# Four tile pools ordered by last use, and an RWKV chunk step in three batches

## The chip, the core and the metric

One core of a Trainium2 chip runs the whole program. The engines are TensorE (PE, with PEld for its weight loads), VectorE (DVE), ScalarE (ACT), GpSimd (POOL) and SyncE (SP, which here issues nearly all DMAs). The metric is the device time of one execution in microseconds; lower is better.

## What is computed

One layer of a bidirectional hybrid trunk, first for a prompt of 256 tokens and then for 2048 latent tokens, in float32:

```python
h = rms_norm(x, p['norm_mix_g']) * (1.0 + scale1) + shift1
(r, k, v, wd_f, wd_b, ad_f, ad_b, gd, xb, gb, q, ff, fb, iv, og) = jnp.split(h @ p['w_in'], idx, axis=-1)
o_a, s_a = rwkv7_mixer(r, k, v, (wd_f, wd_b), (ad_f, ad_b), gd, s_rwkv, p)   # 8 heads of 64, forward + backward
o_b, s_b = rglru_mixer(xb, gb, s_lru, p)
o_c, s_c = hgrn2_mixer(q, (ff, fb), iv, og, s_hgrn, p)
x = x + gate1 * (jnp.concatenate([o_a, o_b, o_c], axis=-1) @ p['w_out'])
h = rms_norm(x, p['norm_ffn_g']) * (1.0 + scale2) + shift2
x = x + gate2 * conv_ffn(h, p, on_grid)          # gated MLP, width-3 depthwise convolution

# inside rwkv7_mixer, per direction and token
s_kk = jnp.einsum('bhvk,bhk->bhv', S, kk_t)
S = (S * w_t[:, :, None, :] - s_kk[..., None] * (kk_t * a_t)[:, :, None, :] + v_t[..., None] * k_t[:, :, None, :])
o_t = jnp.einsum('bhvk,bhk->bhv', S, r_t)
```

The latent tokens start from cached states, the prompt from zero; outputs are both token sets (final RMSNorm) and the prompt's final states.

## The kernel before, in words

The 2304 tokens are 9 pieces of 256: piece 0 is the prompt. **Phase 1** (`dense1`) projects five sections of two pieces (the last has one) with w_in: each weight block of 128 columns is split in a high and a low part (`split`, line 364 on ACT and line 365 on POOL or DVE), and three matmuls (lines 368 to 370, helper `mm3`) make one float32 product. Between its steps a list of lanes runs: generators that issue a few instructions up to their next `yield`. `run` adds a rate per lane to a credit at each step of the dense generator and steps the lane once for each full credit (`RATES` in phase 1, `RATES2` during the prompt's MLP). Lane 1 holds the forward RWKV chain (`rw_fwd`), then the prompt's backward chain and its tail; lane 5 holds the backward chain of pieces 8 to 6; lane 0 the per-head preparation and later the tails (`rw_tail`: group norm, gate, and a store of the mixed rows to DRAM as dMX). Lane 4 solves the triangular systems of a section (`rw_solve`).

An RWKV chunk is 64 tokens for 8 heads (4 pairs). `rw_loads` reads its operands: ar (two buffers), bk and tt (one buffer each), uv (two). `rw_chunk` then runs five batches, each ended by a yield: the Gram matmuls of bk with ar and their masking into gm (lines 743 to 750; the copy at line 747 on POOL); the transposes of bk (line 756), copied to bt by ACT; z (line 768); u (line 775); the new state (line 782, DVE lines 784 and 785) with the output (lines 789 to 796). `in_order` keeps the PE instructions of one chunk in this order. The operands of the next chunk are loaded at the beginning of a chunk. There are 36 forward and 36 backward chunks; those of the prompt's and the latent pieces 8 to 6 run before the second phase, the backward chunks of pieces 5 to 1 inside it, on lane 0 at rate 1. In the backward chain of pieces 8 to 6 the tiles go by other names (`ALT`: ar is k, bk is r, uv is v, gm is hft1, bt is est), and their PSUM tiles too.

Then the prompt's output projection and MLP run (`dense2([(0, 1)])`, with DN["late"] set), and **phase 2**, `dense2(SEC2)`, does the same for pieces 6 to 8, 3 to 5 and 1 to 2. For a section of three pieces the tokens are two halves of 384. Each half loads the mixed rows (`mixin`, m<-dMX, line 1436), the rows of x (`xin`, line 1446) and, quarter by quarter, w_out (`rows_w`, line 1453), which DVE multiplies by the gate g1 (line 1455) and which is split; products are added to x at line 1479.

Instruction order is fixed when the program is built: a scheduler places instructions on each engine's queue by priority and by a simulated time line, and a tile's memory is waited for tile by tile. Pools are stacks from two sides. On the right, phase 1 has cp1, mpa and mpb (the tags of `LATE` go to mpb); after them phase 2 puts gp2 (gate g1), ha2 (high, low and x tiles of the first half), wp2 (split weights, three deep) and rp2 (raw weights and m, three deep) over the same memory. On the left stand the weights and tiles of the prompt's MLP, and then hp2 (gates g2 and fg, MLP tiles), mp2 and hb2 of phase 2.

Of the kernel before, what the change touches and what calls it, by code (L numbers as in the profile page):

```python
# [10 lines left out]
F32 = mybir.dt.float32  # L11
# [46 lines left out]
RATES = (1.2, 1.0, 0.8, 0.6, 0.8, 1.2)  # L58
RATES2 = (1.5, 2.0, 2.0, 1.0, 2.0, 3.0)
# [42 lines left out]
def build(tc, a, o):  # L102
# [9 lines left out]
    NCH = NT // 64  # L112
# [296 lines left out]
    cp, mpa, mpb = [pool(p1, nm, "right") for nm in ("cp1", "mpa", "mpb")]  # L409
    lp = pool(pd1, "lp1", "left")  # L410

    class mp:

        LATE = {"AR", "BK", "t1", "t2", "t3", "hft0", "gst", "gs2", "gs3", "k", "r", "v", "hft1", "est", "hg1", "hH0",
                "S1", "kk", "t4", "lw0", "lw1", "la0", "la1"}

        @staticmethod
        def tile(shape, dt, tag, bufs, name):
            return (mpb if tag in mp.LATE else mpa).tile(shape, dt, tag=tag, bufs=bufs, name=name)

# [307 lines left out]
    def rw_chunk(bp, d, c, ld, Sin, emit_o, tg={}):  # L728

        def tl(tag, shape):  # L730
            tag, bufs = tg.get(tag, (tag, 1))
            return bp.tile(shape, F32, tag=tag, bufs=bufs, name=tag)
# [4 lines left out]
        ar, bk, tt, uv = ld  # L737
        H = (slice(0, 64), slice(64, 128))
        last = None
# [5 lines left out]
        gm = tl("gm", [128, 4, 2, 128])  # L745
# [6 lines left out]
        yield  # L752
        pb = [pt("eo"[h], [128, 4, 64]) for h in range(2)]
        for p in range(4):
            for h in range(2):
                last = in_order(last, T.transpose(pb[h][:, p, :], bk[H[h], p, :, :].rearrange("r a x -> r (a x)"),
                                                  ident[H[h], H[h]]))
        bt = tl("bt", [128, 4, 2, 64])
        for h in range(2):
            S.copy(bt[:, :, h, :], pb[h])  # L760
        yield
# [23 lines left out]
        V.tensor_tensor(S1, S1, WC[d][c // 8][:, c % 8, :].unsqueeze(2).to_broadcast([128, 4, 64]), op=ALU.mult)  # L785

# [21 lines left out]
    def rw_fwd(q):  # L808

        yield from until(lambda: (2 * (q // 2), 0) in solved)  # L810
        if q == 0:
            s0 = mp.tile([128, 4, 64], F32, tag="S0", bufs=2, name="S0")
            V.memset(s0, 0.0)
            rwF["S"] = [s0]
            rwF["ld"] = rw_loads(mp, 0, 0)
            yield
        elif q == 1:
            st = rw_state_in(mp, 0)
            rw_final(mp, 0, rwF["S"])
            yield  # L820
            rwF["S"] = [rw_flip(mp, st, "S0")]
            yield
        for ci in range(4):
            c = 4 * q + ci
            ld = rwF["ld"] if rwF.get("ld") else rw_loads(mp, 0, c)
            rwF["ld"] = rw_loads(mp, 0, c + 1) if ci < 3 else None

            def emit_o(po):
                ob = mt("mv", (128, 4, 64), 1)
                S.copy(ob, po)  # L830
                S.dma_start(dOF[q][ci], ob.rearrange("r p x -> r (p x)"))
            yield from rw_chunk(mp, 0, c, ld, rwF["S"], emit_o)
# [416 lines left out]
    def rw_bwd(q):  # L1249
# [15 lines left out]
        ld = rw_loads(BG["pool"], 1, 4 * q + 3, tg)  # L1265
        for ci in (3, 2, 1, 0):
            cur, ld = ld, (rw_loads(BG["pool"], 1, 4 * q + ci - 1, tg) if ci else None)
# [3 lines left out]
            yield from rw_chunk(BG["pool"], 1, 4 * q + ci, cur, rwB["S"], emit_o, tg)  # L1271
# [300 lines left out]
    def dense2(secs, between):  # L1572
# [14 lines left out]
        for i, (q0, n) in enumerate(secs):  # L1587
# [61 lines left out]
            DN.update(ps=both)  # L1649
            bump(part=0)  # L1650
# [137 lines left out]
    gp, ha, wp2, rp2 = [pool(p2, nm, "right") for nm in ("gp2", "ha2", "wp2", "rp2")]  # L1788
# [6 lines left out]
    for nm, j in (("g1", 16), ("g2", 40), ("fg", None)):  # L1795
        DN[nm] = gate_rows([(gp if nm == "g1" else hp2).tile([128, 512], F32, name=f"{nm}{f}") for f in range(2)], j, 1)
# [45 lines left out]
```

## Time and profile before

| what | value |
|---|---|
| median of three runs | 3950.99 us (3948.19 to 3953.86) |
| the profiled execution | 3953.64 us, span of its trace 3951.8 us |
| PE busy | 3652.6 us, 92% of the span |
| DVE, ACT, POOL busy | 2466.2, 1597.5, 1186.0 us |
| mean granted clock of TensorE | 0.959 |

Busy time is the sum over an engine's instructions. A granted clock of 1 is 2.4 GHz and of 0.5 is 1.2 GHz; a value between is the mean of a stretch. "Idle before, releaser" is the time that an engine stood still before an instruction and whose end let it go on. A wait on SP's queue is time in which a DMA issue stood at the head of that queue.

### The profile page before, as it was taken

What the parts mean: (1) busy time and instruction counts of PE and PEld (TensorE: products, weight loads), DVE (VectorE), ACT (ScalarE), POOL (GpSimd) and SP (SyncE); (2) the same over time, 40 slices, a digit from 0 to 9 for tenths busy, and PEclk for the clock granted to TensorE, in tenths of its full rate; (3) what the DMA queues carried; (4) which work ended last, traced back from release to release, by engine and by line L of the source; (5) the groups of instructions that cost most, each with busy time, mean ns of one, the idle gap of its engine ahead of it and who ended that gap; (6) DMA issues with size and microseconds to landing.
All of it is one profiled execution on the core that took longest, in us unless ns stands there. A gap on an engine that the chain in (4) does not pass through costs nothing.

```text
span 3951.8 us, 74642 instructions
## 1 busy us (share of the span) xinstructions
PE 3652.6 (92%) x29752; PEld 3055.7 (77%) x29752; DVE 2466.2 (62%) x4623; ACT 1597.5 (40%) x2840; POOL 1186.0 (30%) x808
## 2 busy tenths in 40 slices
PE   5998999989999997799867999999999999999998
PEld 3776777766777785688746888998778999979998
DVE  4667777576667677856678455353765433376665
ACT  4456345444554656444333222222342222243333
POOL 2441221202021021334433333333333333343332
PEclk8999999989999997899988999999999999999999
DMA  7988977777877888666464232222522222242332
GB/s 255 305 271 267 271 228 242 241 205 212 248 237 221 268 273 255 200 175 190 122 210 128 85 91 78 74 83 65 173 75 64 71 65 65 64 144 81 97 91 81
DMA packets 769538, 649.10 MB, mean 164 GB/s; under 512 B 247258, under 2 KB 647974, under 8 KB 768166
## 3 DMA queue, kind: packets, MB, share of 16 engines
q1 hardware_dynamic: 736790, 610.10, 51.0%
q10 hardware_dynamic: 32400, 34.22, 2.8%
q8 instruction: 235, 3.85, 0.4%
q14 instruction: 113, 0.93, 0.1%
HBM read 481.08 MB, written 163.10 MB: 163 GB/s over the span
## 4 chain that ended last, share of the span: by engine, by line
PE 47%; DVE 7%; DMA 3%; issue 2%; ACT 1%; POOL 0%; SPq 0%; ACTq 0%; DVEq 0%; POOLq 0%
PE mm L368 6%; PE mm L369 6%; PE mm L370 6%; PE xh L368 6%; PE xh L369 5%; PE xh L370 5%; PE e L368 1%; PE e L369 1%; PE e L370 1%; DVE raw L1455 1%; PE o L369 1%; DVE x L1479 1%; PE o L370 1%; PE o L368 1%; DVE tm L1559 1%
## 5 line engine op out<-in xcount | busy, mean ns | idle before, releaser
L365 POOL TENSOR_TENSOR wlo<-raw,whi 128x1024 fp32r<-128x1024 f32 x273 | 666.5, 2443 | 972.5 <-ACT whi L364 680.1
L368 PE MATMUL mm<-hhi,whi 128*128 128x512 f32 (+2 forms) x2224 | 801.5, 361 | 25.2 <-ACT whi L364 8.5
L369 PE MATMUL mm<-hlo,whi 128*128 128x512 f32 (+2 forms) x2224 | 788.8, 355 | 8.0 <-DVE hlo L286 5.6
L370 PE MATMUL mm<-hhi,wlo 128*128 128x512 f32 (+2 forms) x2224 | 785.5, 353 | 2.0 <-DVE wlo L365 1.0
L364 ACT CAST whi<-raw 128x1024 fp32r<-128x1024 f32 x333 | 348.3, 1048 | 717.5 <-PE mm L370 319.2
L368 PEld LDWEIGHTS mm<-hhi,whi 128*128 128x128 f32 x2224 | 427.8, 193 | 84.1 <-issue 13.3
L369 PEld LDWEIGHTS mm<-hlo,whi 128*128 128x128 f32 x2224 | 428.2, 193 | 51.8 <-DVE hlo L286 6.3
L370 PEld LDWEIGHTS mm<-hhi,wlo 128*128 128x128 f32 x2224 | 427.5, 192 | 45.9 <-POOL wlo L365 2.1
L365 POOL TENSOR_TENSOR alo<-gs,ahi 128x384 fp32r<-128x384 f32 (+1 forms) x154 | 150.4, 977 | 445.0 <-ACT ahi L364 431.6
L368 PE MATMUL xh<-hhi,whi 128*128 128x384 f32 (+1 forms) x824 | 274.5, 333 | 4.5 <-ACT hhi L364 4.5
L369 PE MATMUL xh<-hlo,whi 128*128 128x384 f32 (+1 forms) x824 | 272.6, 331 | 3.2 <-DVE hlo L365 2.6
L370 PE MATMUL xh<-hhi,wlo 128*128 128x384 f32 (+1 forms) x824 | 272.6, 331 | 0.0
L1675 DVE SCALAR_TENSOR_TENSOR gs<-xh,vec,gs 128x378 f32<-128x378 f32 (+1 forms) x103 | 60.8, 590 | 318.2 <-ACT gs L1671 318.2
L1479 DVE TENSOR_TENSOR x<-xh,x 128x512 f32<-128x512 f32 x220 | 150.5, 686 | 88.9 <-PE xh L370 85.1
L1479 DVE TENSOR_TENSOR x<-mm,x 128x512 f32<-128x512 f32 x172 | 118.1, 687 | 108.9 <-PE mm L370 107.1
L747 POOL COPY gm<-ar 64x256 f32<-64x256 f32 x120 | 58.2, 485 | 391.5 <-PE c L792 301.4
L1455 DVE TENSOR_TENSOR raw<-raw,g 128x1024 f32<-128x1024 f32 x98 | 127.3, 1299 | 76.3 <-DMA raw<-in_ffn_w_down 67.5
L365 POOL TENSOR_TENSOR t<-t,t 128x512 fp32r<-128x512 f32 (+1 forms) x40 | 53.0, 1325 | 388.0 <-ACT t L364 301.2
L1681 DVE SCALAR_TENSOR_TENSOR gs<-fsg,gs 128x384 f32<-128x384 f32 (+1 forms) x154 | 122.6, 796 | 71.4 <-ACT fsg L1680 71.1
L368 PEld LDWEIGHTS xh<-hhi,whi 128*128 128x128 f32 x824 | 156.0, 189 | 8.0 <-ACT hhi L364 4.8
L369 PEld LDWEIGHTS xh<-hlo,whi 128*128 128x128 f32 x824 | 155.8, 189 | 5.2 <-DVE hlo L365 2.9
L370 PEld LDWEIGHTS xh<-hhi,wlo 128*128 128x128 f32 x824 | 155.9, 189 | 0.7
(607 smaller groups left out, 8415.9 us busy)
## 6 DMA issues: line engine op xcount, KB each, us to landing
whi<-dW SPq DMA_DIRECT2D x116, 512.0 KB
wlo<-dW SPq DMA_DIRECT2D x116, 512.0 KB
raw<-in_ffn_w_gate SPq DMA_DIRECT2D x88, 512.0 KB
raw<-in_ffn_w_up SPq DMA_DIRECT2D x88, 512.0 KB
raw<-in_ffn_w_down SPq DMA_DIRECT2D x88, 512.0 KB
x<-in_x_sample SPq DMA_DIRECT2D x44, 512.0 KB
raw<-in_w_out SPq DMA_DIRECT2D x40, 512.0 KB
dAR<-AR SPq DMA_DIRECT2D x32, 512.0 KB
```

The costliest lines, as they stand in the source:

```text
L364: S.copy(hi, raw)
L365: e.tensor_tensor(lo, raw, hi.bitcast(F32), op=ALU.subtract)
L368: T.matmul(out, whi, xhi, start=first, stop=False)
L369: T.matmul(out, whi, xlo, start=False, stop=False)
L370: T.matmul(out, wlo, xhi, start=False, stop=last)
L747: G.tensor_copy(gm[H[h], :, h, 0:64], ar[H[h], :, 0, :])
L1455: V.tensor_tensor(raw, raw, g[f].unsqueeze(1).to_broadcast([128, 2, 512]), op=ALU.mult)
L1479: V.tensor_tensor(x1b[:, FS[f]], pt, x1b[:, FS[f]], op=ALU.add)
L1559: V.tensor_scalar(t[:, 128 * i:128 * i + 128], pt[:, 128 * i:128 * i + 128], A2[:, k, c:c + 1], mod[:, 24 + k, c:c + 1], op0=ALU.mult, op1 ...
L1675: V.scalar_tensor_tensor(gv[:, :, 1:rw], pv[:, :, 0:rw - 1], cw(0), gv[:, :, 1:rw], op0=ALU.mult, op1=ALU.add)
L1681: V.scalar_tensor_tensor(gs[:, :w], sg[:, :w], 1.0, gs[:, :w], op0=ALU.add, op1=ALU.mult)
```

## The change

- The pools of phase 1 on the right become cp1, mpa (`EARLY`), mpd (`JOIN`), mpc (`CHAIN`) and mpb (the rest). Phase 2's right-hand pools are opened in the order gp2, rp2, wp2, ha2.
- The gates g2 and fg of phase 2 are loaded by `mlp_gates`, called after the first output projection of phase 2; g1 is loaded where it was.
- A chunk step has three batches: transposes, S copies and z; u; new state, the Gram of the next chunk (`rw_gram` on the head `nxt`), output. The first chunk of a chain, or one whose successor's section is not solved when it begins, has its Gram in a batch of its own. `nxt` may belong to the next piece, except in phase 2.
- The transposes are four of 128 by 128 into one PSUM bank, copied by one ACT instruction, instead of eight of 64 rows into two banks and two copies.
- The rates of lanes 1 and 5 are three fifths of what they were.

```diff
-RATES = (1.2, 1.0, 0.8, 0.6, 0.8, 1.2)
-RATES2 = (1.5, 2.0, 2.0, 1.0, 2.0, 3.0)
+RATES = (1.2, 0.6, 0.8, 0.6, 0.8, 1.2)
+RATES2 = (1.5, 1.2, 2.0, 1.0, 2.0, 1.8)
...
-    cp, mpa, mpb = [pool(p1, nm, "right") for nm in ("cp1", "mpa", "mpb")]
+    cp, mpa, mpd, mpc, mpb = [pool(p1, nm, "right") for nm in ("cp1", "mpa", "mpd", "mpc", "mpb")]
...
+        EARLY = {"ar", "bk", "tt", "uv", "gm", "bt", "mv", "S0", "Dn", "m4", "hq", "ep", "hg0", "hS", "nss", "ls", "lhl"}
+        JOIN = {"hK", "hQ", "hF", "hA", "hH1", "hl", "hVt", "hv", "hg64"}
+        CHAIN = {"k", "r", "v", "hft1", "est", "hg1", "hH0", "S1"}
...
-            return (mpb if tag in mp.LATE else mpa).tile(shape, dt, tag=tag, bufs=bufs, name=name)
+            p = mpa if tag in mp.EARLY else mpd if tag in mp.JOIN else mpc if tag in mp.CHAIN else mpb
+            return p.tile(shape, dt, tag=tag, bufs=bufs, name=tag)
...
+    def rw_head(bp, d, c, tg={}):
+
+        return {"ld": rw_loads(bp, d, c, tg), "c": c}
...
+    def rw_turn(bp, hd, last, tg):
+
+        tl, pt = rw_tiles(bp, tg)
+        bk = hd["ld"][1]
+        pb = pt("e", [128, 4, 128])
+        for p in range(4):
+            last = in_order(last, T.transpose(pb[:, p, :], bk[:, p, :, :].rearrange("r a x -> r (a x)"), ident))
+        hd["bt"] = tl("bt", [128, 4, 2, 64])
+        S.copy(hd["bt"].rearrange("r p h x -> r p (h x)"), pb)
+        return last
+
+    def rw_gram(bp, d, hd, last, tg):
...
-        yield
-        pb = [pt("eo"[h], [128, 4, 64]) for h in range(2)]
-        for p in range(4):
-            for h in range(2):
-                last = in_order(last, T.transpose(pb[h][:, p, :], bk[H[h], p, :, :].rearrange("r a x -> r (a x)"),
-                                                  ident[H[h], H[h]]))
-        bt = tl("bt", [128, 4, 2, 64])
-        for h in range(2):
-            S.copy(bt[:, :, h, :], pb[h])
-        yield
+        return last
+
+    def rw_chunk(bp, d, hd, nxt, Sin, emit_o, tg={}):
...
+        if "gm" not in hd:
+            last = rw_gram(bp, d, hd, last, tg)
+            yield
+        last = rw_turn(bp, hd, last, tg)
+        gm, bt = hd["gm"], hd["bt"]
         S0 = Sin[0]
...
         V.tensor_tensor(S1, S1, WC[d][c // 8][:, c % 8, :].unsqueeze(2).to_broadcast([128, 4, 64]), op=ALU.mult)
+        if nxt is not None:
+            last = rw_gram(bp, d, nxt, last, tg)
 
         po = pt("c", [128, 4, 64])
...
+            if i == 0 and not DN["late"]:
+                mlp_gates()
             bump(part=0)
...
-    gp, ha, wp2, rp2 = [pool(p2, nm, "right") for nm in ("gp2", "ha2", "wp2", "rp2")]
+    gp, rp2, wp2, ha = [pool(p2, nm, "right") for nm in ("gp2", "rp2", "wp2", "ha2")]
...
-    for nm, j in (("g1", 16), ("g2", 40), ("fg", None)):
-        DN[nm] = gate_rows([(gp if nm == "g1" else hp2).tile([128, 512], F32, name=f"{nm}{f}") for f in range(2)], j, 1)
+    DN["g1"] = gate_rows([gp.tile([128, 512], F32, name=f"g1{f}") for f in range(2)], 16, 1)
+
+    def mlp_gates():
+        for nm, j in (("g2", 40), ("fg", None)):
+            DN[nm] = gate_rows([hp2.tile([128, 512], F32, name=f"{nm}{f}") for f in range(2)], j, 1)
```

## Rows read from the trace of the kernel before

**Rows 1.** Busy time by stage (length, busy us per engine, granted clock, DMA share, GB/s)
```profile
100.00:1500.00 1400.00, 1305.53 (x13252) 1013.77 (x13251) 990.35 (x2059) 712.67 (x1353) 293.99 (x237) 0.96 0.82 249
1700.00:1950.00 250.00, 242.20 (x2750) 209.60 (x2750) 158.12 (x279) 110.25 (x200) 116.25 (x90) 1.00 0.59 172
2200.00:2840.00 640.00, 634.75 (x3854) 553.61 (x3853) 312.58 (x499) 187.10 (x302) 224.38 (x138) 0.99 0.30 92
```

**Rows 2.** PE in order of time (start, duration, instruction) at the phase boundary
```profile
1968.22 0.39 PE L370 MATMUL mm<-whi,alo 128*128 128x512 f32 x1
...
2004.37 1.22 PE L368 MATMUL xh<-whi,hhi 128*128 128x512 f32 x2
```

**Rows 3.** Busy time by stage, the boundary (columns PE, PEld, DVE, ACT, POOL)
```profile
1968.00:2004.00 36.00, 6.27 (x31) 4.33 (x29) 18.43 (x35) 11.50 (x19) 7.26 (x4) 0.59 0.70 207
2004.00:2120.00 116.00, 92.66 (x784) 68.09 (x786) 99.43 (x174) 37.29 (x73) 46.09 (x28) 0.91 0.53 161
```

**Rows 4.** Waits on SP's queue, 1900 to 2220 us (total, times, longest)
```profile
SPq L1470 <- DVE x L1505: 24.8, 1, 24.8
```

**Rows 5.** SP's DMA issues in order of time
```profile
1787.99 0.92 SPq L1470 DMA_DIRECT2D g<-dG  x2
...
1976.07 0.94 SPq L1470 DMA_DIRECT2D g<-dG  x2
...
1982.01 6.07 SPq L1436 DMA_DIRECT2D m<-dMX  x3
```

**Rows 6.** ACT and DVE in order of time: last uses of phase 1's tiles
```profile
1785.63 0.37 ACT L830 COPY mv<-c 128x256 f32<-128x256 f32 x1 [2.38 <-PE c L796]
...
1935.49 0.37 ACT L1270 COPY AR<-x 128x256 f32<-128x256 f32 x1 [1.44 <-PE x L796]
...
1982.25 0.87 DVE L1311 SCALAR_TENSOR_TENSOR t<-t,lnbP,x 128x256 f32<-128x256 f32 x2 [1.12 <-PE x L1309]
```

**Rows 7.** The chain that ended last, a load of bk (start, duration)
```profile
2076.29 4.31 DMA bk<-dBK
```

**Rows 8.** DVE groups by line, 2013 to 2120 us (busy, mean ns, idle before)
```profile
L1455 DVE TENSOR_TENSOR raw<-raw,g 128x1024 f32<-128x1024 f32 x12 | 14.8, 1236 | 0.0
```

**Rows 9.** Line 782 alone by stage (first PE count is its instructions)
```profile
400.00:1540.00 1140.00, 25.23 (x496) 19.25 (x496) 0.95 0.80 240
...
1700.00:1950.00 250.00, 11.67 (x256) 9.24 (x256) 1.00 0.59 172
...
2200.00:3100.00 900.00, 11.86 (x224) 8.82 (x224) 0.99 0.29 86
```

**Rows 10.** PE in order of time; left out are the transposes: L756, then four of L1300
```profile
2397.03 0.39 PE L370 MATMUL xh<-whi,alo 128*128 128x512 f32 x1
2397.26 0.40 PE L368 MATMUL xh<-whi,ahi 128*128 128x512 f32 x1
...
2397.79 0.50 PE L369 MATMUL xh<-wlo,ahi 128*128 128x512 f32 x1
2398.13 0.40 PE L370 MATMUL xh<-whi,alo 128*128 128x512 f32 x1
...
2398.84 0.50 PE L368 MATMUL mm<-whi,ahi 128*128 128x512 f32 x1
...
3078.16 0.34 PE L370 MATMUL mm<-hhi,wlo 128*128 128x384 f32 x1
3078.33 0.34 PE L368 MATMUL mm<-hhi,whi 128*128 128x384 f32 x1
...
3078.86 0.42 PE L369 MATMUL mm<-hlo,whi 128*128 128x384 f32 x1
```

**Rows 11.** PE in order of time, transposes and state matmuls of one forward chunk
```profile
1462.41 0.27 PE L756 MATMUL e<-ident,bk 64*128 64x64 f32 x1
...
1471.76 0.69 PE L782 MATMUL c<-uv,bt 128*64 128x64 f32 x16
```

**Rows 12.** Waits on SP's queue, 2200 to 3100 us
```profile
SPq L1408 <- POOL wlo L365: 338.7, 53, 15.1
```

More of the change, by code (lines that the diff above doesn't have):

```diff
@@ L736, in pt @@
             return ps(tag, shape, bufs)
-        ar, bk, tt, uv = ld
-        H = (slice(0, 64), slice(64, 128))
-        last = None
+        return tl, pt
+    RH = (slice(0, 64), slice(64, 128))
+    def rw_turn(bp, hd, last, tg):
[8 more added lines that the diff above has]
+    def rw_gram(bp, d, hd, last, tg):
+        tl, pt = rw_tiles(bp, tg)
+        ar, bk = hd["ld"][:2]
+        H = RH
         pg = [pt("eo"[h], [128, 4, 128]) for h in range(2)]
@@ L744, in rw_chunk @@
                                                ar[H[h], p, :, :].rearrange("r a x -> r (a x)"), start=True, stop=True))
-        gm = tl("gm", [128, 4, 2, 128])
+        gm = hd["gm"] = tl("gm", [128, 4, 2, 128])
         for h in range(2):
@@ L751, in rw_chunk @@
                             rkm[d][:, 64:128].unsqueeze(1).to_broadcast([128, 4, 64]), op=ALU.mult)
-        yield
-        pb = [pt("eo"[h], [128, 4, 64]) for h in range(2)]
-        for p in range(4):
-            for h in range(2):
-                last = in_order(last, T.transpose(pb[h][:, p, :], bk[H[h], p, :, :].rearrange("r a x -> r (a x)"),
-                                                  ident[H[h], H[h]]))
-        bt = tl("bt", [128, 4, 2, 64])
-        for h in range(2):
-            S.copy(bt[:, :, h, :], pb[h])
-        yield
+        return last
+    def rw_chunk(bp, d, hd, nxt, Sin, emit_o, tg={}):
+        tl, pt = rw_tiles(bp, tg)
+        H, c = RH, hd["c"]
+        ar, bk, tt, uv = hd["ld"]
+        last = None
+        if "gm" not in hd:
[3 more added lines that the diff above has]
+        gm, bt = hd["gm"], hd["bt"]
         S0 = Sin[0]
@@ L824, in rw_fwd @@
             c = 4 * q + ci
-            ld = rwF["ld"] if rwF.get("ld") else rw_loads(mp, 0, c)
-            rwF["ld"] = rw_loads(mp, 0, c + 1) if ci < 3 else None
+            hd = rwF.pop("hd", None) or rw_head(mp, 0, c)
+            nxt = None
+            if c + 1 < NCH and (ci < 3 or q and (2 * ((q + 1) // 2), 0) in solved):
+                nxt = rwF["hd"] = rw_head(mp, 0, c + 1)
             def emit_o(po):
@@ L831, in emit_o @@
                 S.dma_start(dOF[q][ci], ob.rearrange("r p x -> r (p x)"))
-            yield from rw_chunk(mp, 0, c, ld, rwF["S"], emit_o)
+            yield from rw_chunk(mp, 0, hd, nxt, rwF["S"], emit_o)
         fwd_done["rw"].add(q)
@@ L1264, in rw_bwd @@
         on = rwB["on", q] = nt(f"on{q % 2}", (128, 4, 4, 64), 1)
-        ld = rw_loads(BG["pool"], 1, 4 * q + 3, tg)
         for ci in (3, 2, 1, 0):
-            cur, ld = ld, (rw_loads(BG["pool"], 1, 4 * q + ci - 1, tg) if ci else None)
+            c = 4 * q + ci
+            hd = rwB.pop("hd", None) or rw_head(BG["pool"], 1, c, tg)
+            nxt = None
+            if ci or q > SEC2[0][0] and (2 * ((q - 1) // 2), 1) in solved:
+                nxt = rwB["hd"] = rw_head(BG["pool"], 1, c - 1, tg)
             def emit_o(po):
                 S.copy(on[:, ci], po)
-            yield from rw_chunk(BG["pool"], 1, 4 * q + ci, cur, rwB["S"], emit_o, tg)
+            yield from rw_chunk(BG["pool"], 1, hd, nxt, rwB["S"], emit_o, tg)
         if q == 0:
```

5 lines of the change are left out of this document (1 added, 4 removed).

## Prediction

> **What bounds the kernel now.** I read the busy time by stage first, then the stretch in which TensorE (PE) is least busy, then who frees the memory and the queue that this stretch waits for. From 100 to 1500 us, while the input projection runs, PE is busy 1305.5 of 1400 us; from 1700 to 1950 it is busy 242.2 of 250, and from 2200 to 2840 634.8 of 640 [rows 1]. There a microsecond of PE work saved is nearly a microsecond off the end. The hole is the boundary between the prompt's MLP and the second phase: the prompt's last dense matmul starts at 1968.22 and the first dense matmul of the second phase at 2004.37 [rows 2]. From 1968 to 2004 PE is busy 6.27 of 36 us and its granted clock is 0.59, the mean of a stretch that is mostly at 1.2 GHz; from 2004 to 2120 VectorE (DVE) is busy 99.4 of 116 us and PE 92.7 [rows 3]. So the boundary is idle time with a cause outside the engines, and behind it comes a stage that DVE limits.
>
> The cause stands on SP's queue. A gate load (line 1470) sat at its head for 24.8 us until the prompt's last add (line 1505) [rows 4]; it went at 1976.07, the mixed activations m<-dMX only at 1982.01 [rows 5]. Two things held them. First, gates g2 and fg lie in hp2 on the left, over buffers of the prompt's MLP, and are issued ahead of all loads of the second phase. Second, the raw weight ring rp2 is the last of four right-hand pools and lies over the first tiles of mpb, which the last tail still reads: its last DVE step is at 1982.25 [rows 6]. That memory and not data is the limit shows in what did get through: g1, over memory that had come free, was loaded at 1787.99, 180 us before the prompt's last dense matmul [rows 5].
>
> **Part 1, pools and late gates.** The new order puts gp2, rp2 and wp2 (40 KB a partition by their shapes) over cp1 and EARLY (about 40 KB), whose last user is the forward chunk chain: its last output copy is at 1785.63 [rows 6]. The weights of w_out can then be loaded and split under the prompt's MLP. ha2 (hi, lo and x of the first half) moves to the worse place, over JOIN and the first part of CHAIN; CHAIN's last readers are the backward chunks, the last of which is copied out at 1935.49 [rows 6]. So the first half can be ready some 30 us ahead of 1968.22. mlp_gates takes four loads off the head of SP's queue and puts them behind the output projection; behind them stand MLP weights with a ring of three, so I cost them at nothing (if they came late, the first w_down multiply would wait for one landing, and the nearest landing in the trace, of bk, is 4.31 us [rows 7]).
>
> What goes: of the 36 us, 6.27 us is PE work that stays (tail, Gram). 29.7 us is the most that the hole gives. DVE sets how much of it stays: 18.4 + 99.4 = 117.8 us of DVE work lie between 1968 and 2120 [rows 3]. At the 86% that it reaches from 2004 on those need 137 us instead of 152. The first three gate multiplies of raw weights and three splits of activations, some 1.24 us each [rows 8], can run before 1968: an estimate of 7.4 us, which leaves 110.4 us of DVE work, or 128 us at 86%, 24 less than now. A gain of 28 asks for 110.4 in 124 us, 89%, which the weights loaded early make likely. I take **28 us**, with 10 as the lower end (most of the early start is given back to DVE) and 45 as the upper (the whole hole, and in addition the half-speed clock gone and the PE holes of the prompt's last 15 us filled).
>
> **Part 2, the chunk step.** There are 9 x 4 x 2 = 72 chunk steps; line 782 issues 16 PE instructions in each, which puts 31 in 400 to 1540, 16 in 1700 to 1950, 14 in 2200 to 3100 [rows 9], and the other 11 in stages that PE does not limit. Removed per step: eight 64-row transposes (line 756), two ACT copies, two yields. Added: four 128-row transposes into one bank, one ACT copy. Price where PE is full: in a stream of dense matmuls 0.23 us apart (2397.03 to 2397.26), one half transpose put 2397.79 - 2397.26 = 0.53 us, the other seven 2398.84 - 2398.13 = 0.71; less two steps of 0.23 that is 0.78 us [rows 10]. Four full transposes (line 1300) between matmuls 0.17 us apart (3078.16 to 3078.33) put 3078.86 - 3078.33 = 0.53, so 0.36 us [rows 10]. The saving is **0.42 us a step**. The Gram of the next chunk moves from a batch of its own to between the state and the output matmuls; the scheduler could already place it there, for it depended on loads alone, so I take 0 for that, with 0.3 (the price of one more interruption of the dense stream, 0.53 - 0.23 [rows 10]) as the upper end and a loss of 0.2 as the lower.
>
> The Trainium skill, TensorEngine Tiling (Array Packing), Performance Considerations, speaks against this edit: with a contraction of 64 rows, two row tiles run side by side, so packed transposes should be no dearer than whole ones. By that the 0.42 would be nothing. The same page, Tiling Modes, says that a change of the mode drains the engine; the 0.30 us for a single transpose agrees with it.
>
> The sum: 31 x 0.42 x 0.7 (PE is 93% busy there and some of the saving falls into other waits; my choice) = 9.1; 16 x 0.42 = 6.7; 14 x 0.42 = 5.9; together **22 us**. The chunk's recurrent chain (copy of S, z, u, S) keeps its steps, so the 11 others give 0. The saved ACT copy is hidden.
>
> **Part 3, rates.** Five yields at 1.0 and three at 0.6 are the same 0.2 chunks per dense step; 2.0/5 = 1.2/3 and 3.0/5 = 1.8/3. Steps that are not chunks on these lanes (tail 0, state flips, the first Gram of a piece) run slower, under a full PE: 0. In the second phase the rate stays 1, so chunks come 5/3 as fast: some four more of them fall before 2200, PE work out of a full stage into one with holes, but DVE work into the stage that DVE limits. I take 0, plus or minus 8.
>
> **New waits.** gm has one buffer, so the next Gram's masks on DVE and its copy on POOL queue behind the output matmuls of the current step; before they did too. The new tie is on PE: the output matmuls stand, in order, behind the next chunk's Gram, and that behind the load of bk, which has one buffer and is freed by the transposes of the same step.
>
> **Rivals.**
> 1. Only the boundary gains: the full transposes, each 128 columns long, cost as much as the packed ones once they stand in one batch with z. For it: the 0.78 holds a split batch, an unsplit one is cheaper. Then 3951 - 28 = 3923. The packing rule of the skill would give the same.
> 2. The wait moves: hi, lo and x of the first half now wait for the backward chain (1935.49 [rows 6]), and if that slips towards 1960, or DVE gives the start back, 10 us of 28 stay: 3951 - 10 - 22 = 3919.
> 3. Both upper ends: 45 + (31 x 0.7 + 16 + 14) x 0.72 = 82, so 3869.
> 4. It does not do what it says: the second phase still starts at the last tail, and the scheduler spreads the batches as before: 3951, within 0.2%.
> 5. Slower: PE stalls behind bk. From the transposes to the state matmuls one step has 1471.76 - 1462.41 = 9.3 us [rows 11]; bk lands 4.31 us after its issue [rows 7], and SP's queue is held 338.7 / 53 = 6.4 us at a time by raw weights (2200 to 3100, longest 15.1) [rows 12]. 10.7 us against 9.3 decides against the change; each step would stall PE 1.4 us, 72 of them 101 us, less 50: 4002. Against it: most steps have more room, and the scheduler places a late Gram later.
>
> **How the numbers follow.** The profiled run took 3953.64 us with a span of 3951.8; the median of the runs is 3950.99, 2.65 less. 28 + 22 = 50: span 3901.8, such a run 3903.6, median **3901**. Chances: forecast 0.50 (itself 3885 to 3917), rival 1 0.15, rival 2 0.13, rival 3 0.08, rival 4 0.06, rival 5 0.08. Range 3862 to 3945: it takes in the first four cases and the plus or minus 8 of the rates, and leaves out rivals 4 and 5. A measurement here tells about 0.2% (8 us) from no change: faster 0.86, same 0.06, slower 0.08.
>
> **What would show it.** Right: loads of w_out under the prompt's MLP, well before 1950; no long wait of line 1470 on SP; dense second-phase matmuls within some 5 us of the prompt's last; the transposes at four a step with about 0.36 us each time. Wrong: the hole still there with another releaser; DVE at 95% or more and PE as idle as before up to 2200; waits of the Gram or output matmuls for bk in most chunk steps; the chunk count before 1500 lower than now, with the forward chain ending later.

## The result, and the profile after

| | before | after | ratio (95% interval) |
|---|---|---|---|
| first series, medians of 4 runs | 3952.43 us (3948.19 to 3955.03) | 3906.36 us (3904.16 to 3923.15) | 0.9895 (0.9871 to 0.9919) |
| second series (after_again below) | 3958.31 us (3954.65 to 3965.58) | 3907.83 us (3902.86 to 3911.14) | 0.9866 (0.9851 to 0.9880) |
| the profiled execution, span | 3951.8 us | 3904.7 us | |

The forecast was 3901 us. The change takes 46 to 50 us off; the forecast's sum was 50. What follows shows where it comes off, since one of the two sums came out through another mechanism than the one it was made for.

One thing about the views first. Busy time of a group counts each moment once, however many of the group's instructions run in it; it is not simply the sum over them, as the note to the table of the kernel before says. Instructions of two groups can run at the same moment, so their busy times must not be added. This matters for the chunk step below.

Busy time by stage of the kernel after, the stages of [rows 1] and [rows 3] (length, busy us of PE, PEld, DVE, ACT, POOL, granted clock, DMA share, GB/s):

```profile
100.00:1500.00 1400.00, 1306.67 (x13203) 1015.73 (x13202) 1002.52 (x2096) 725.20 (x1345) 300.63 (x240) 0.97 0.83 250
1700.00:1950.00 250.00, 237.20 (x2669) 206.56 (x2666) 162.18 (x278) 109.14 (x186) 118.19 (x89) 0.99 0.60 176
2200.00:2840.00 640.00, 634.99 (x3850) 554.75 (x3849) 318.38 (x520) 186.18 (x290) 223.95 (x142) 1.00 0.31 94
1968.00:2004.00 36.00, 28.43 (x103) 21.80 (x104) 24.00 (x42) 12.54 (x20) 12.72 (x7) 0.80 0.30 96
2004.00:2120.00 116.00, 87.92 (x749) 66.16 (x747) 95.71 (x186) 39.78 (x76) 36.26 (x25) 0.86 0.61 182
```

The stages that were full are still full. The hole is not: from 1968 to 2004 PE works 28.43 us instead of 6.27, at a clock of 0.80 instead of 0.59. SP's issues in order of time show why:

```profile
1888.93 0.99 SPq L1468 DMA_DIRECT2D m<-dMX  x2
...
1925.48 1.38 SPq L1478 DMA_DIRECT2D x<-in_x_sample  x3
1930.73 32.72 SPq L1485 DMA_DIRECT2D raw<-in_w_out  x8
1963.50 1.01 SPq L1502 DMA_DIRECT2D g<-dG  x2
...
1976.46 0.38 SPq L1485 DMA_DIRECT2D raw<-in_w_out  x1
2014.47 1.47 SPq L1468 DMA_DIRECT2D m<-dMX  x3
2015.99 4.04 SPq L1478 DMA_DIRECT2D x<-in_x_sample  x3
```

The mixed rows of the first half go out at 1888.93, where they went at 1982.01 before [rows 5]; the weights of w_out follow from 1930.73, under the prompt's MLP. So the first dense matmul of phase 2 runs before the prompt's last (PE in order of time):

```profile
1940.43 1.22 PE L368 MATMUL xh<-whi,hhi 128*128 128x512 f32 x2 [0.94 <-ACT whi L364]
...
1950.15 0.40 PE L370 MATMUL mm<-whi,alo 128*128 128x512 f32 x1
```

In [rows 2] the same two stand at 2004.37 and 1968.22. What is late next shows in the last lines of SP: m and x of the second half go at 2014.47 and 2015.99. The tail of piece 6 writes the last rows that m reads. Its last DVE step, at 1982.25 before [rows 6], comes at 2000.88 here (DVE in order of time):

```profile
2000.88 0.87 DVE L1343 SCALAR_TENSOR_TENSOR t<-t,lnbP,x 128x256 f32<-128x256 f32 x2
```

DVE was full shortly before: it multiplies the weights that now come early (line 1487) and adds phase 2's first products (line 1511) beside the prompt's last ones, and PE waits for it (a PE instruction, then busy time from 1950 to 1970, columns as above):

```profile
1967.75 0.80 PE L368 MATMUL xh<-whi,hhi 128*128 128x512 f32 x1 [5.63 <-DVE x L1511]
```
```profile
1950.00:1970.00 20.00, 10.20 (x32) 7.12 (x31) 20.00 (x23) 4.34 (x9) 9.72 (x5) 0.80 0.42 138
```

To say where the 47 us come off, one mark is needed that doesn't move with the schedule. I count dense matmuls (lines 368 to 370) and compare the start of the n-th with that of the n-th in the kernel before. The kernels of the experiments stand in the same table; each row is the lead (minus) or lag in us of one profiled execution, and the first row has the time before.

```
n               2200     3300     3960     4840     5280     6600     9240    13900
before        1014.7   1442.0   1751.9   1949.3   2184.8   2489.4   3109.9   3909.4
after          -14.6     -3.1    -42.8    -19.6    -37.7    -35.4    -48.8    -47.1
after_again    -12.1     -1.7    -39.7    -11.4    -31.5    -28.9    -44.0    -44.4
gates_first    -12.3     -2.4    -43.6    -18.8    -36.4    -33.4    -49.0    -46.1
old_order2      -6.0      3.3    -32.5     -3.4    -27.3    -25.0    -39.6    -38.1
old_rates       22.1     -4.5    -24.7      9.8    -26.3    -23.4    -37.9    -37.5
two_pools      -11.4     -1.0    -36.7     -7.9      4.8     -1.5    -16.5    -14.3
chunk_only      -6.9      8.5    -30.2     -2.6      3.1     -3.6    -17.7    -16.6
half_turn        4.0     11.3     -7.6     18.1    -13.7     -9.2    -20.8    -20.1
five_batches    -9.7    -10.1    -22.6      2.8    -30.9    -28.5    -34.8    -34.3
own_gram         2.7     13.5     11.5     27.9      7.8     20.9     16.7     16.6
pools_only       3.9     -1.2      1.9      8.6    -34.4    -14.3    -15.9    -13.1
turn_only      -12.4    -12.0    -21.2      5.6      7.0      7.3      2.1      2.5
```

Three stretches are to be read: up to n = 4840 (the first phase and the prompt's MLP), 4840 to 6600 (the boundary and the work that it puts off) and 6600 to 9240 (phase 2). Dense matmuls alone are counted, so a lead can also be chunk work put off: most of the leads at 3960 are gone at 4840, and from 4840 to 5280 the kernel before does 7 chunk steps (Gram matmuls divided by 16), the changed one 6 and pools_only 5. From 4840 to 6600 every kernel of the table does 13, and from 6600 to 9240 every one does 7, so these two can be compared. The changed kernel gains 15.8 and 13.4 us in them (after_again 17.5 and 15.1) and has 11 to 20 us from before them.

The error of a lead is large. The profiled executions lie up to 10 us from their kernel's median. And the execution before in the table took 3953.64 us, while the kernel before had a median of 3963 us beside eight of the experiments and of 3958 beside the other four: their last column can read 5 to 10 us too small. The verdicts rest on the ratios.

### The profile page after: what moved, and what is told of

Its sections match the earlier page's. It is cut to its first block, busy times and chain, and to the rows that moved or that the text cites. A ratio compares the mean times of both kernels' runs of the same rounds, so it can differ in the third digit from the quotient of the medians.

```text
span 3904.7 us, 74036 instructions
## 1 busy us (share of the span) xinstructions
PE 3632.5 (93%) x29464; PEld 3056.0 (78%) x29464; DVE 2451.9 (63%) x4623; ACT 1592.8 (41%) x2768; POOL 1184.8 (30%) x808
## 4 chain that ended last, share of the span: by engine, by line
PE 59%; DVE 14%; DMA 8%; ACT 4%; issue 3%; POOL 1%; SPq 1%; ACTq 0%; DVEq 0%; POOLq 0%
PE mm L368 9%; PE mm L369 8%; PE mm L370 8%; PE xh L368 6%; PE xh L369 5%; PE xh L370 5%; DVE Dn L634 1%; DVE m L636 1%; DVE raw L1487 1%; DVE x L1511 1%; PE c L794 1%; PE e L368 1%; DMA raw<-in_w_out 1%; PE e L369 1%; PE e L370 1%
```

## The experiments

All ratios are to the kernel before, run beside each kernel; an interval is about 0.002 either way, so a difference of two ratios is sure to some 0.003 (12 us). Line numbers are those of each kernel, and edits are against the changed kernel unless the text says otherwise.

### The boundary: pools, their order, the gates

**pools_only** has the four pools, the new order of phase 2's pools and the late gates, with the chunk step and rates as before (edit against the kernel before):

```diff
-    cp, mpa, mpb = [pool(p1, nm, "right") for nm in ("cp1", "mpa", "mpb")]
+    cp, mpa, mpd, mpc, mpb = [pool(p1, nm, "right") for nm in ("cp1", "mpa", "mpd", "mpc", "mpb")]
...
+            if i == 0 and not DN["late"]:
+                mlp_gates()
...
-    gp, ha, wp2, rp2 = [pool(p2, nm, "right") for nm in ("gp2", "ha2", "wp2", "rp2")]
+    gp, rp2, wp2, ha = [pool(p2, nm, "right") for nm in ("gp2", "rp2", "wp2", "ha2")]
...
```

> The kernel before with the four pools, the new order of the second phase's pools and the late gates; chunk step and rates as before. My theory (boundary worth some 28 us, of which 25 showed between the prompt's last down matmul and the first gate matmul of the second phase): 20 to 30 us faster than before, all of it after 1950 us, and the end of the prompt's MLP within 3 us of before. Rival (the parts only work together, because the earlier end of the backward chain is what lets the second phase start): under 10 us. Rival (the boundary is worth nearly everything, and the 18 us gained ahead of it are a shift in the scheduler's order that any edit of the pools gives): 40 us or more.

3934.69 us, ratio 0.9922 (0.9900 to 0.9944): some 31 us. The table puts it at the boundary: 8.6 behind at n = 4840, 34.4 ahead at 5280, 14.3 ahead at 6600. What is lost again by 6600 is chunk work put off, 8 steps against 6. Over both stretches, with 13 steps each, the gain is 22.9 us.

**two_pools** puts the first phase's tiles back into mpa and mpb, and leaves the rest of the change:

```diff
-            p = mpa if tag in mp.EARLY else mpd if tag in mp.JOIN else mpc if tag in mp.CHAIN else mpb
+            p = mpb if tag in mp.LATE else mpa
```

> The changed kernel with the first phase's tiles back in the two old pools; phase 2's pool order, the late gate rows and the chunk step stay. Theory (four pools and the new order carry the boundary together, each useless alone): the first w_out matmul of phase 2 comes back to 30 to 36 us after the prompt's last down matmul instead of 10 before it, and the ratio to the kernel before is that of the chunk step alone, 0.991 (0.9892 to 0.9932). Rival (the order of phase 2's pools carries it, the four pools add nothing): as the changed kernel, 0.9876 to 0.9895. Rival (something in between): the first loads of w_out early, x or mixin late, 0.990.

3939.47 us, ratio 0.9931 (0.9907 to 0.9955): 26 us worse than the changed kernel (after_again, 0.9866), and no better than the chunk step alone. From n = 4840 to 6600 it loses 6.4 us where the changed kernel gains 15.8. A wait on SP's queue and the PE rows around the boundary say where it hangs now:

```profile
SPq L1480 <- DMA out_y_prompt<-kk: 21.0, 1, 21.0
```
```profile
1952.19 0.40 PE L370 MATMUL mm<-whi,alo 128*128 128x512 f32 x1
...
1998.96 1.22 PE L368 MATMUL xh<-whi,hhi 128*128 128x512 f32 x2 [14.29 <-ACT whi L364]
```

With the new order and the old two pools, the x rows of the first half (line 1480) lie over a tile from which the prompt's output is stored; the hole is 47 us wide.

**old_order2** keeps the four pools and opens phase 2's in the old order:

```diff
-    gp, rp2, wp2, ha = [pool(p2, nm, "right") for nm in ("gp2", "rp2", "wp2", "ha2")]
+    gp, ha, wp2, rp2 = [pool(p2, nm, "right") for nm in ("gp2", "ha2", "wp2", "rp2")]
```

> The changed kernel with phase 2's four right-hand pools in the old order (g1, activations, weights, raw); the four pools of phase 1 stay. Theory (both halves are needed): raw weights of w_out lie over what the forward chunks and the tail use last, so they are issued only after the tail, some 40 us later; first w_out matmul 30 us after the prompt's last down; ratio 0.991, that of the chunk step alone. Rival (four pools are enough): 0.9876 to 0.9895.

3910.32 us, ratio 0.9864 (0.9844 to 0.9885): as the changed kernel. With the old order m goes later (SP in order of time), and the weights still come ahead of the prompt's last matmul:

```profile
1943.03 1.65 SPq L1468 DMA_DIRECT2D m<-dMX  x3
1950.10 34.46 SPq L1485 DMA_DIRECT2D raw<-in_w_out  x8
```

**gates_first** loads g2 and fg where they were loaded before, with all the rest of the change:

```diff
-            if i == 0 and not DN["late"]:
-                mlp_gates()
...
+    for nm, j in (("g1", 16), ("g2", 40), ("fg", None)):
+        DN[nm] = gate_rows([(gp if nm == "g1" else hp2).tile([128, 512], F32, name=f"{nm}{f}") for f in range(2)], j, 1)
```

> The changed kernel with all six gate loads of the second phase up front, as before. My theory (the late gates take 24.8 us of waiting off SP's queue): 10 to 25 us slower than the changed kernel, with line 1499 or 1502 at the head of SP's queue until the prompt's last adds and the first w_out load behind it. Rival (the pool order alone frees the loads, the scheduler puts the gates behind what is ready): within 6 us of the changed kernel.

3914.51 us, ratio 0.9876 (0.9858 to 0.9895): no difference. SP in order of time shows that the scheduler puts the gates behind the weights by itself, once the weights have memory:

```profile
1931.51 37.52 SPq L1485 DMA_DIRECT2D raw<-in_w_out  x8
1969.08 1.01 SPq L1502 DMA_DIRECT2D g<-dG  x2
```

So the boundary's gain is the split of the first phase's tiles into four pools by last use; with it, neither the order above nor the late gates carry anything that can be measured. A kernel with the four pools and both of these taken back at once was not run.

### The chunk step: turn, joined Gram, rates

**chunk_only** has the new chunk step and rates, with pools and gates as before:

```diff
-    cp, mpa, mpd, mpc, mpb = [pool(p1, nm, "right") for nm in ("cp1", "mpa", "mpd", "mpc", "mpb")]
+    cp, mpa, mpb = [pool(p1, nm, "right") for nm in ("cp1", "mpa", "mpb")]
...
```

> The kernel before with the three-batch chunk step, the full transposes and the new rates; pools, their order and the gates as before. My theory (0.42 us of PE work less in each step, where PE is full): 16 to 24 us faster, of it 12 to 18 by the end of the prompt's MLP and 5 to 8 in the second phase, with PE busy time down by 15 to 25 us. Rival (the 18 us ahead of the boundary come from the stretch around 1500 us, where latency and not PE work sets the pace): the gain is there, but in one step between 1440 and 1570 us and not spread over 500 to 1500. Rival (nothing without the pools): within 8 us of before.

3930.87 us, ratio 0.9912 (0.9892 to 0.9932): 35 us alone. With the pools' 31 that would make 66, and the whole change gives 46 to 50; by the last column of the table the two would make only 30. Whether the parts add up can't be told from this.

**turn_only** has the kernel before with nothing changed but the transposes, four whole ones and one copy (edit against the kernel before):

```diff
-        pb = [pt("eo"[h], [128, 4, 64]) for h in range(2)]
+        pb = pt("e", [128, 4, 128])
         for p in range(4):
-            for h in range(2):
...
+            last = in_order(last, T.transpose(pb[:, p, :], bk[:, p, :, :].rearrange("r a x -> r (a x)"), ident))
...
```

> The kernel before with four full transposes and one copy in the place of eight half ones and two copies; five batches and old rates. My theory: the transposes carry the chunk part's gain, 72 steps at 0.42 us, of which 22 reach the end: 15 to 24 us faster, and a group of transposes costs 0.36 us in the dense stream. Rival (merging of batches carries it): under 8 us. Rival (the packing rule): no gain, and a group costs 0.7 us or more.

3966.40 us, ratio 1.0006 (0.9995 to 1.0016): nothing. The edit on which the forecast had put all its 22 us moves the time by itself not at all.

**own_gram** has the changed kernel with the Gram always in a batch of its own, four batches a chunk and the rates at four fifths:

```diff
-RATES = (1.2, 0.6, 0.8, 0.6, 0.8, 1.2)
+RATES = (1.2, 0.8, 0.8, 0.6, 0.8, 1.2)
...
-            yield from rw_chunk(mp, 0, hd, nxt, rwF["S"], emit_o)
+            yield from rw_chunk(mp, 0, hd, None, rwF["S"], emit_o)
...
```

> The changed kernel with the Gram matrices of a chunk always in a batch of their own (four batches, lane rates at four fifths), so no chunk's Gram follows the state of the chunk before. The whole transposes, the pools and the gates stay. Theory A (joining the next chunk's Gram to the state update is what shortens the chunk step, and the turn nothing): the chunk step's 35 us (ratio 0.9912 alone) go, and what stays is the pools' part, 0.992; the step of 20 us at 1440 to 1570 us isn't there. Rival B (the joined batch is worth nothing; fewer and later switches between dense and chunk work, by the rates, carry it): in between, 0.9885 to 0.991. Rival C (neither: the turn with its one copy): no change from the changed kernel, 0.9876 to 0.9895.

3975.81 us, ratio 1.0032 (1.0019 to 1.0045): theory A went too short. Not only is the chunk step's gain gone, the pools' is too.

**five_batches** is the cleaner version: the Gram and the turn each in a batch of their own, the old rates, and the whole transposes, pools and gates of the change:

```diff
...
+        yield
         gm, bt = hd["gm"], hd["bt"]
...
-            yield from rw_chunk(mp, 0, hd, nxt, rwF["S"], emit_o)
+            yield from rw_chunk(mp, 0, hd, None, rwF["S"], emit_o)
...
```

> The changed kernel with the Gram never joined to the chunk before, the turn in a batch of its own, and the old lane rates: the old five batches with the whole transposes, the new pools and gates. It tells the join apart from the crowding of the four-batch kernel. Theory (the join carries the chunk step's gain, the turn nothing): the pools' part alone, ratio 0.992 to 0.994, as the kernel with the pools alone (0.9922) times the turn alone (1.0006). Rival A (the four-batch kernel measured the join rightly, 1.6 per cent): 1.000 to 1.003. Rival B (the join is worth little and the four-batch kernel lost by waits of its own): 0.987 to 0.990.

3925.24 us, ratio 0.9916 (0.9898 to 0.9935): the theory's value, that of the pools alone. So taking out the join costs 20 us, and own_gram lost another 45 by its own four-batch form.

**half_turn** keeps the join and takes the transposes back to eight halves:

```diff
-        pb = pt("e", [128, 4, 128])
+        pb = [pt("eo"[h], [128, 4, 64]) for h in range(2)]
...
```

> The changed kernel with the turn as before: eight 64-row transposes into two PSUM tiles and two copies a chunk instead of four whole ones and one copy. Theory (the turn's saving, which alone gave nothing, gives nothing here either): within 0.2 per cent of the changed kernel. Rival A (the forecast's term: 0.42 us a chunk on PE, 61 chunks, most of it in PE time): 20 to 26 us more, ratio up by 0.005 to 0.0065. Rival B (the single PSUM tile makes the solve wait for the copy, and two halves don't): up to 10 us less.

3940.47 us, ratio 0.9946 (0.9930 to 0.9961): 32 us worse than the changed kernel. In time this is Rival A and more than it asked for, but not for its reason, as the rows below show: the turn that is worth nothing without the join is worth 32 us with it.

With the pools of the change there are now all four combinations:

| | half transposes | whole transposes |
|---|---|---|
| Gram in its own batch | 0.9922 (pools_only) | 0.9916 (five_batches) |
| Gram joined | 0.9946 (half_turn) | 0.9866 (after_again) |

Neither edit gains alone; the two together gain 20 to 22 us. The joined kernels have three batches and the new rates, the others five and the old ones. old_rates (below) excludes the rates; the number of batches was not told apart from the join.

A part of the mechanism shows in PE's groups of Gram and transposes up to 1990 us (shapes, count, busy us, mean ns, idle before and its releaser), which belong to the same 40 chunk steps in each kernel. Before:

```profile
L743 PE MATMUL o<-ar,bk 64*128 64x128 f32 x320 | 55.3, 306 | 0.0
L743 PE MATMUL e<-ar,bk 64*128 64x128 f32 x320 | 54.0, 303 | 2.8 <-DVE m L679 2.2 <-DVE m L664 0.6
L756 PE MATMUL e<-ident,bk 64*128 64x64 f32 x160 | 25.1, 249 | 9.1 <-DVE gm L750 7.1 <-DVE m L664 1.8
L756 PE MATMUL o<-ident,bk 64*128 64x64 f32 x160 | 20.2, 243 | 0.6 <-DVE gm L750 0.3
```

The whole turn in five batches (five_batches):

```profile
L765 PE MATMUL o<-ar,bk 64*128 64x128 f32 x320 | 56.1, 308 | 0.0
L765 PE MATMUL e<-ar,bk 64*128 64x128 f32 x320 | 55.4, 307 | 6.5 <-DVE m L682 3.6 <-DMA bk<-dBK 1.7 <-issue 1.2
L753 PE MATMUL e<-ident,bk 128*128 128x128 f32 x160 | 26.2, 288 | 8.2 <-DVE m L667 5.6 <-DVE gm L772 2.5
```

The join with half transposes (half_turn):

```profile
L768 PE MATMUL o<-ar,bk 64*128 64x128 f32 x320 | 51.5, 296 | 0.0
L768 PE MATMUL e<-ar,bk 64*128 64x128 f32 x320 | 50.8, 295 | 0.0
L754 PE MATMUL e<-ident,bk 64*128 64x64 f32 x160 | 27.3, 258 | 22.7 <-DVE gm L775 17.2 <-DVE m L667 5.5
L754 PE MATMUL o<-ident,bk 64*128 64x64 f32 x160 | 20.6, 249 | 1.6 <-DVE gm L775 1.5
```

Both, the changed kernel:

```profile
L765 PE MATMUL o<-ar,bk 64*128 64x128 f32 x320 | 52.1, 297 | 0.0
L765 PE MATMUL e<-ar,bk 64*128 64x128 f32 x320 | 51.4, 296 | 0.0
L753 PE MATMUL e<-ident,bk 128*128 128x128 f32 x160 | 27.0, 294 | 11.3 <-DVE gm L772 10.9 <-DVE m L667 0.3
```

The groups named e and o run side by side. These are four of the seven half transposes that stand between 2398.13 and 2398.84 of [rows 10] (PE of the kernel before, in order of time):

```profile
2398.45 0.27 PE L756 MATMUL o<-ident,bk 64*128 64x64 f32 x1
2398.46 0.27 PE L756 MATMUL e<-ident,bk 64*128 64x64 f32 x1
2398.57 0.22 PE L756 MATMUL o<-ident,bk 64*128 64x64 f32 x1
2398.57 0.22 PE L756 MATMUL e<-ident,bk 64*128 64x64 f32 x1
```

So the two may not be added. Busy time of all PE instructions that read bk, which are these groups together, up to 1990 us (length, PE, PEld, granted clock, DMA share, GB/s; in order before, five_batches, half_turn and after):

```profile
0.00:1990.00 1990.00, 87.96 (x960) 65.50 (x960) 0.94 0.77 234
0.00:1990.00 1990.00, 87.73 (x800) 67.36 (x800) 0.95 0.78 236
0.00:1990.00 1990.00, 84.27 (x960) 62.88 (x960) 0.94 0.78 235
0.00:1990.00 1990.00, 82.63 (x800) 63.92 (x800) 0.95 0.78 237
```

With the idle time of the groups, divided by 40, a step's Gram and turn take of PE, in us:

| kernel | busy, together | idle before Gram, turn | a step | ratio |
|---|---|---|---|---|
| before | 87.96 | 2.8, 9.7 | 2.51 | 1 |
| pools_only | 88.19 | 2.6, 8.9 | 2.49 | 0.9922 |
| five_batches | 87.73 | 6.5, 8.2 | 2.56 | 0.9916 |
| half_turn | 84.27 | 0.0, 24.3 | 2.71 | 0.9946 |
| own_gram | 89.29 | 6.8, 17.5 | 2.84 | 1.0032 |
| old_rates (below) | 84.00 | 2.9, 10.7 | 2.44 | 0.9872 |
| after | 82.63 | 0.0, 11.3 | 2.35 | 0.9895, 0.9866 |

The whole transposes save almost no PE time: the busy time of the transposes alone, counted in the same way over these 40 steps, is 27.7 us before and 27.0 in the changed kernel. With the 12 backward steps before 1990 us, whose tiles have other names, it is 35.69 and 34.67 us, 0.02 a step (line 756 before, line 753 after):

```profile
0.00:1990.00 1990.00, 35.69 (x416) 23.08 (x416) 0.94 0.77 234
0.00:1990.00 1990.00, 34.67 (x208) 25.00 (x208) 0.95 0.78 237
```

The join is what shortens the rows: the Gram's busy time, counted in the same way, is 60.2 us before, 54.4 in half_turn and 55.7 in the changed kernel, and the wait before it is gone. The half transposes then lose more than this. In the joined kernel they stand where DVE has not yet masked the Gram (gm), and wait 24.3 us in all, where they waited 9.7 before; the whole ones wait 11.3. Together the two edits take 0.16 us a step off, where the join with half transposes adds 0.20. That the whole turn waits less because it uses one of the two PSUM tiles of the Gram and the halves use both is argued, not shown.

The sum puts the kernels in nearly the order of their times, but it isn't the time. Over 72 steps the 0.36 us between half_turn and after would be 26 us of the 32 measured, and the 0.21 between five_batches and after 15 of 20. own_gram has 0.35 more than pools_only, 25 us of the 41 by which it is slower; its chain rows wait longer too (for uv at the new state 16.5 us in all against 12.5 in the kernel before, for the copied z at u 8.2 against 1.4). The rest of its loss stays open.

In phase 2 the whole turn does pay by itself, since there the scheduler cuts the eight halves apart. Before, the transposes of 14 steps stand in 30 pieces, ten of them a single half; the whole ones of turn_only stand in 15 pieces. One of these pieces (PE of turn_only in order of time):

```profile
2405.04 0.40 PE L368 MATMUL xh<-whi,ahi 128*128 128x512 f32 x1
2405.28 0.60 PE L755 MATMUL e<-ident,bk 128*128 128x128 f32 x4
2405.64 0.51 PE L369 MATMUL xh<-wlo,ahi 128*128 128x512 f32 x1
```

Four whole ones put 0.60 us between two dense matmuls here, the single half of [rows 10] 0.53. Counted from start to start like this, less 0.23 for each piece, a step's transposes cost 0.77 us before and 0.44 in turn_only in phase 2, and 0.62 and 0.56 in the 40 steps of the first phase (an estimate: there nearly half of the pieces have no dense matmul before them).

From n = 6600 to 9240 all seven kernels with the join and the whole turn (after, after_again, gates_first, old_order2, old_rates, two_pools, chunk_only) gain 13.4 to 15.6 us over their 7 steps. The join with half transposes gains 11.6, the whole turn without join 4.2 to 6.3 (own_gram, turn_only, five_batches), and the old step 1.6 (pools_only). The join's 10 us aren't all its own: before, 920 PE instructions other than dense matmuls and transposes lie in the stretch, in the changed kernel 854, so some work of the lanes has moved out of it.

**old_rates** has the changed kernel with the old lane rates:

```diff
-RATES = (1.2, 0.6, 0.8, 0.6, 0.8, 1.2)
-RATES2 = (1.5, 1.2, 2.0, 1.0, 2.0, 1.8)
+RATES = (1.2, 1.0, 0.8, 0.6, 0.8, 1.2)
+RATES2 = (1.5, 2.0, 2.0, 1.0, 2.0, 3.0)
```

> The changed kernel with the old lane rates: three batches a chunk, but at the pace of five, so a chunk takes three fifths of the dense steps it took. Theory A (the batch's content carries, and the pace was only kept): no difference within 0.3% of the changed kernel, 0.987 to 0.992, with the rwkv lanes ending earlier and the rest unchanged. Rival B (pace matters: chunks that come faster than their loads and VectorE steps make PE wait): some 16 chunks with 1 to 2 us more of waiting each, 20 to 30 us, ratio 0.994 to 0.997. Rival C (a chunk's chain is late in phase 1b, and more pace ends it sooner): 0.984 to 0.987.

3912.81 us, ratio 0.9872 (0.9855 to 0.9889): nothing. The road is another one (at n = 2200 it is 22.1 behind, where the changed kernel is 14.6 ahead, and at 4840 it is 9.8 behind), the end is the same. The rate of lane 5 in phase 1 is 1.2 in both kernels; three fifths hold for its rate during the prompt's MLP.

### The changed kernel beside them, and what is late next

**after_again** is the changed kernel without an edit.

> The changed kernel itself, beside the others on one chip. Theory: 0.987 to 0.989 here, as the three kernels that differ from it in the late gates, the order of phase 2's pools and the rates (0.9864 to 0.9876), so that these three parts are worth nothing. Rival: 0.9895, its ratio on the other chip, and each of the three loses a little for the change.

3907.83 us, ratio 0.9866 (0.9851 to 0.9880): the theory. The late gates (0.9876), the order of phase 2's pools (0.9864) and the rates (0.9872) carry nothing that can be measured.

**tail_in_hot** gives m and x of the second half priority in the schedule, and the draining of the lanes too:

```diff
-    lanes.drain()
+    with tc.high_priority(HP):
+        lanes.drain()
...
-                    hh[h] = mixin(q0, h, h0, w)
+                    if i == 0 and h and not DN["late"]:
+                        with tc.high_priority(HP):
+                            hh[h] = mixin(q0, h, h0, w)
+                    else:
+                        hh[h] = mixin(q0, h, h0, w)
...
```

> The changed kernel with the loads of the first section's second half in phase 2 (its mixer output and x rows) put ahead in the schedule, and the draining of the lanes at the end of the prompt too. Theory (what is late next after the boundary is the second half's inputs behind the backward chunk's loads on SP's queue): the loads start 8 to 10 us sooner and up to 10 us come off, ratio down by 0.001 to 0.0025. Rival A (the tail of piece 6 sets it, whose last write to the mixer output ends at 2002 us): no change. Rival B (the queue stands behind the loads that wait for the tail, and the other work of phase 2 is late): 5 to 15 us more.

3919.42 us, ratio 0.9897 (0.9882 to 0.9911): 12 us worse, as rival B had it. Its SP queue in order of time:

```profile
1987.33 0.38 SPq L1485 DMA_DIRECT2D raw<-in_w_out  x1
2015.23 0.93 SPq L1468 DMA_DIRECT2D m<-dMX  x2
...
2021.87 0.58 SPq L724 DMA_DIRECT2D ar<-dAR  x1
```

m stands ahead of the chunk's loads now, and goes at 2015.23, not earlier than without priority. For some 27 us nothing is issued. The wait on SP's queue names what m waits for, the tail's store of the mixed rows:

```profile
SPq L1468 <- DMA dMX<-t: 27.3, 1, 27.3
```

The chunk's loads, which went between 1985.62 and 2013.64 in the changed kernel, start at 2021.87. At n = 5280 the kernel is 42.2 ahead, at 6600 only 23.7. So m of the second half doesn't stand behind the queue; it waits for its data, as rival A had it, and the chunk's loads were right to go first. No version was found that beats the changed kernel: old_order2, old_rates and gates_first lie within its interval.

## Why the prediction was right, and where it was not

**The boundary, 28 us: right in size and place.** pools_only gives 31 by its ratio, two_pools against the changed kernel 26; in the table pools_only gains 22.9 from n = 4840 to 6600. The mechanism held: memory and not data was the limit of [rows 5], the weights of w_out came under the prompt's MLP, and phase 2's first dense matmul starts 9.7 us ahead of the prompt's last. Three details failed. The cause was put on two things, the gates at the head of SP's queue [rows 4] and the ring rp2 over tiles in use [rows 6]; gates_first shows that the gates were a follower, since with free memory the scheduler issues them after the weights. "The new order puts gp2, rp2 and wp2" over EARLY gave the credit to the order; old_order2 shows that the old order over the four pools does as well. And the step by which the 28 was chosen, DVE going from 86% to 89%, did not happen. Take the same 199 dense matmuls in both kernels, which start from 1968.2 to 2121.6 before and from 1946.0 to 2074.4 after: DVE is busy 119.1 of 153.3 us before and 101.6 of 128.4 after, 78% and 79%. The share stayed, and 17.5 us of DVE work lie outside the stretch now. Some 6 of these are the work that the sum moved ahead with 7.4, gate multiplies (19.7 us before, 17.6 after) and splits of activations (7.5 and 3.7); most of the rest is work of the lanes, with 4 chunk steps in the stretch instead of 6. DVE did hold something back, by the mechanism of rival 2 if not at its size: it is full from 1950 to 1970, the tail of piece 6 ends 18.6 us later than before, and the second half starts after it.

**The chunk step, 22 us: the total right by luck, its step wrong.** The pools alone against the whole change (0.9922 to 0.9866) give 22 us, sure to some 10; against the kernel before the chunk step alone gives 35. The sum put 0.42 us a step on the transposes and 0 on the Gram, and both terms failed. The 0.42 was the price of a split batch among dense matmuls [rows 10]. In phase 2 it nearly holds: 0.77 less 0.44 is 0.33 a step, 4.6 us over 14 steps, where 5.9 were forecast. In the first phase the transposes' busy time falls by 0.02 us a step, by starts some 0.06, and turn_only (1.0006) gains nothing: the terms of 9.1 and 6.7 us had no saving behind them. The other failed step is the sentence that took 0 for the Gram because "the scheduler could already place it there". It wasn't there: with the Gram in a batch of its own PE waited 2.8 us before it in the first phase and its rows took 60.2 us, joined 0.0 and 55.7. Joined, and only with the whole turn, it is worth the 20 to 22 us. So two errors offset each other: the turn's 16 us of the first phase were not there, and the gain of join and turn together was missing. How this gain is spread over the first phase can't be read from the table: at n = 4840 kernels with this step lie between 19.6 ahead and, in old_rates, 9.8 behind.

**Rates, 0: right.** old_rates 0.9872 against 0.9866.

**The rivals.** Rival 1 (only the boundary gains) had the right reason for the first phase: in busy time the whole transposes cost there what the packed ones cost. What it left out is the join, which makes the whole ones pay. The Trainium skill (TensorEngine Tiling (Array Packing), Tiling Modes) says that different tiles can run their matmuls in parallel. The trace agrees: 320 halves of 246 ns would last 78.7 us one after another and took 27.7 of busy time, and the 160 whole ones took 27.0. Rival 4 is excluded by the rows of the boundary. Rival 5 (PE behind the load of bk) didn't happen: the changed kernel's Gram rows show no wait for it, 0.0 us over 640 matmuls, and the longest total in a joined kernel is 2.0 us, in old_rates.

## What to carry to other kernels

When a stage cannot start, look at whose memory its loads lie over; here one regrouping of tiles by last use carried the boundary, and the order and the late loads put beside it did nothing that could be measured. Two edits of one step can be worth nothing or less alone and some 20 us together, if one sets what the other waits for: test each without the other in both directions before a gain is put down to one. Before busy times of two groups are added, look in the order of time whether they run side by side. And a price read from one place holds for that place: 0.42 us a step came from a split batch in phase 2, and in the first phase next to nothing of it was there.

## What was not expected of the hardware

A single half transpose among dense matmuls costs nearly what four whole ones cost: 0.53 us from dense start to dense start [rows 10] against 0.60, where a step is 0.23. In one batch, two halves side by side take 0.17 us of busy time (27.7 / 160) and one whole transpose 0.17 (27.0 / 160), for the same data. A Gram matmul takes 302 to 312 ns where the Gram is a batch of its own, and 295 to 301 in the joined kernels, except in old_rates, where it takes 308 and 310; why old_rates differs is open. And single executions of one program differ from the median by up to 17 us (3923.15 against 3906.36), yet the gain from n = 6600 to 9240 repeats within 2.2 us in the seven kernels with the same chunk step.
